# Strassen sums of x by accumulating DMA with one token half kept negative, memory's gains folded into ScalarE's rounding, and early loads issued at the start

## Chip, cores and metric

One core of one Trainium2 chip. The metric is device time in microseconds of one execution; lower is better. The kernel before took 919.43 us (median of 3 runs, 918.79 to 920.02).

## The reference, cut to what matters

One layer of a streaming encoder over 544 tokens (512 of a prompt, 32 of a running stream), width 2048, all in float32:

```python
h = rmsnorm(x, g_norm); proj = h @ w_in          # 2048 -> 6656
rq, rk, rv, rg, gu, gv, gg, aq, ag = split(proj)
ro = groupnorm(retention(rope(rq), rope(rk), rv)) * silu(rg)
go = gu * (tril(w_s) @ layernorm(gv) + b_s) * silu(gg)
ao = softmax(aq @ mem_k.T) @ mem_v * silu(ag)
out = x + concat([ro, go, ao]) @ w_out;  y = rmsnorm(out, g_final)
mem_k, mem_v = split(rmsnorm(mem_prompt, g_mem) @ w_mem_kv)   # 256 memory tokens
```

The memory's keys and values, the retention states and the normalised gate rows are outputs too.

## The kernel before, in words

Every large product is float32 by parts: an operand is split into an upper part, rounded to the matmul type (ScalarE, `copy`, L87), and a lower part, the remainder (VectorE, `tt`, L90); three matmuls (upper by upper, upper by lower, lower by upper) make one term. PE, DVE, ACT, POOL and SP are TensorE, VectorE, ScalarE, GpSimd and the sync engine's DMA queue.

The input projection runs by pairs of 128-column weight slices (`PAIRS`, L34: xa0 to xa3, then qk and vg by heads, gv, gg), the output projection as o0 to o7. Each pair is a 2 by 2 block product: K in two halves of 8 tiles, two weight slices, two halves of 272 tokens. xa0 and o0 do it with eight products (`plain`, L323); all others with seven (Strassen's form, `project`, L237), which needs four sums of the x blocks (S1 = 21 + 22, S3 = 11 - 21, S2 = S1 - 11, S4 = 12 - S2; block gi is token half g, K half i) and four sums of the weight blocks (`sources`, L173). One product is 24 matmuls of 272 columns (`multiply`, L221). A weight's two parts lie in tags `whi` and `wlo` with three buffers each; `ahead` (L209) makes the lower part of the next weight and begins (upper part) the one behind it.

Up to the end of xa0 the order on PE, DVE and ACT is the program's order by hand: `put` (L82) pins each instruction behind what was traced on its engine, until `fixed[0] = False` (L573). DMA starts are not pinned. After that the tile scheduler orders by readiness.

The stages before the first pair:

- Loads on SP (L407 to L412): memory tokens `mem` and key weights `wk` in pieces. The rest is issued between the key units, each behind the release of a buffer of the tag `raw` (three buffers): key piece 3, the constant table `ct`, the token-major x `xt` (only for its sums of squares), value weights `wv`, then x feature-major (`x`, L354, from `xT`), and xa0's weights (`load_half`, L166).
- Keys (L443 to L474): for 8 units, DVE multiplies memory by its gains (`gains_mem`, L416), ACT rounds weights and memory, DVE makes the remainders, ACT squares the memory (L432), PE does 24 matmuls.
- Values (L479 to L543): 8 units of 12 matmuls of 512 columns. In between, the sums of squares of memory and x become factors (`token_factors`, L292, with a power on POOL), spread over the partitions by diagonal matmuls (`rm_ps`, `r_ps`), copied to `rm_bc` and `r_bc`.
- x: `scale_x` (L524) multiplies each K tile by gain and token factor; `split_x` (L528) and `block` (L400) split the blocks into `A11`, `A21`, `A12`, `A22`.
- xa0 (`plain` with `between`, L553): the sums of x are DVE instructions over 128 x 2176 elements, at j = 3 and 5 and, for S4, in `last_sums` (L577). Block S2 follows at j = 5, S1 at j = 7; S3 and S4 in `last_sums`. ACT copies the results to `Xxa` (`pair`), from which head 0's scores `sc` are made (L601).

Of the kernel before, what the change touches and what calls it, by code (L numbers as in the profile page):

```python
# [8 lines left out]
F32 = mybir.dt.float32  # L9
# [5 lines left out]
P = 128  # L15
# [61 lines left out]
def step_kernel(ctx: ExitStack, tc: tile.TileContext, a, o):  # L77
# [95 lines left out]
    def sources(name, key):  # L173
# [12 lines left out]
        if key == "t3":  # L186
# [7 lines left out]
            f"o{NO - 1}": ("11", "21", "t2", "t1", "22", "t3", "t4")}  # L194
    units = [(n, key) for n in ORDER for key in FOUR.get(n, SEVEN)]
    begun, done = [], [0]

    def begin():

        if len(begun) < len(units):  # L200
            name, key = units[len(begun)]
            load_half(ORDER.index(name), 0)
            load_half(ORDER.index(name), 1)
            src = sources(name, key)
            u = unit(f"{name}{key}")
            copy(u[0], src)
            begun.append((src, u))

    def ahead():  # L209

        if done[0] < len(units):
            if done[0] == len(begun):
                begin()
            name, key = units[done[0]]
            src, u = begun[done[0]]
# [119 lines left out]


    with tc.tile_pool(name="mkv", bufs=1, reuse_waits="tile") as mkv, ExitStack() as ctx_x:
# [3 lines left out]
        with tc.tile_pool(name="pa", bufs=1, reuse_waits="tile") as pa:  # L341
            mem = [ap.tile([P, KS, MEM], F32, tag=f"12{u}", name=f"mem{u}") for u in "hl"]
            mg = [ap.tile([P, KS, MEM], F32, tag=f"22{u}", name=f"mg{u}") for u in "hl"]
# [3 lines left out]
            xk = [ap.tile([P, KS, T], F32, tag="S4", name="x0"), pb.tile([P, KS, T], F32, name="x1")]  # L347
# [5 lines left out]
            def load_x(k0, k1):  # L353
                nc.sync.dma_start(out=xk[k0 // KS][:, k0 % KS:k0 % KS + k1 - k0], in_=a["xT"][:, k0:k1])  # L354

            def load_kv(which, q, pieces=1):
                r = wp.tile([P, 4, 512], F32, tag="raw", name=f"{which}{q}", bufs=3)
# [54 lines left out]
            load_mem(12, 16)  # L412
            put(nc.vector.memset(ssx, 1.0))


            def gains_mem(u):  # L416
                if u < 8:
                    i, ks = u // 4, slice(u % 4 * 2, u % 4 * 2 + 2)
                    tt(mg[i][:, ks], mem[i][:, ks], gm[:, 2 * u:2 * u + 2].unsqueeze(2).to_broadcast([P, 2, MEM]), ALU.mult)

            ku = {}

            def key_unit(u):
                if u < 8:
                    i, ks = u // 4, slice(u % 4 * 2, u % 4 * 2 + 2)
                    w, src = unit(f"k{u}", [P, 2, 512]), wk[u // 2][:, u % 2 * 2:u % 2 * 2 + 2]
                    copy(w[0], src)
# [4 lines left out]
                    put(nc.scalar.activation(out=mem[i][:, ks], in_=mem[i][:, ks], func=AF.Square))  # L432
                    ku[u] = w

            vu, wv = {}, []
# [6 lines left out]
            gains_mem(0)  # L442
            key_unit(0)  # L443
            for u in range(8):
                key_unit(u + 1)
                if u == 5:
                    part0 = halve(mem[0], KS)
                elif u == 6:
                    value_unit(0)
                elif u == 7:  # L450
                    part1 = halve(mem[1], KS)
                    value_unit(1)
                    square_x(0)
                for k in range(2 * u, 2 * u + 2):
# [4 lines left out]
                if u == 1:  # L459
                    wk.append(load_kv("wk", 3))  # L460
                    nc.sync.dma_start(out=ct, in_=a["table"][:, 0:K_COS])
                    for t in (0, 1, 4):
                        load_tokens(t)
                elif u == 3:
                    wv.append(load_kv("wv", 0))
                    for t in (2, 3):
                        load_tokens(t)
                elif u == 5:
                    wv.append(load_kv("wv", 1))
                elif u == 7:  # L470
# [16 lines left out]
            square_x(1)  # L487
# [31 lines left out]
            copy(r_bc, ps[:, 0:T])  # L519
            value_unit(7)  # L520
            value(5)
            load_half(0, 1)

            def scale_x(i, k0, k1):  # L524
                for k in range(k0, k1):
                    stt(xk[i][:, k], xk[i][:, k], gn[:, KS * i + k:KS * i + k + 1], r_bc, ALU.mult, ALU.mult)

            def split_x(i, k0, k1):  # L528
                if k0 == 0:
                    new_block(f"1{i + 1}", "A")  # L530
                h = A[f"1{i + 1}"]
                split(h[0][:, k0:k1], h[1][:, k0:k1], xk[i][:, k0:k1, 0:TH])

            scale_x(0, 0, 4)
            split_x(0, 0, 4)
            value(6)
            scale_x(0, 4, 8)
# [6 lines left out]
            nc.sync.dma_start(out=o["cache_v"].rearrange("(m p) c -> p m c", p=P), in_=mv_p)  # L544
            put(nc.vector.tensor_scalar(out=gret, in0=gret, scalar1=0.5, scalar2=None, op0=ALU.mult))
            block("21", xk[0][:, :, TH:T])
# [4 lines left out]
            h11, h21, h12, h22 = xk[0][:, :, 0:TH], xk[0][:, :, TH:T], xk[1][:, :, 0:TH], xk[1][:, :, TH:T]  # L551

            def between(j):  # L553
# [514 lines left out]
def laid_out(i):  # L1068
# [21 lines left out]
    r["xT"] = feature_major(np.concatenate([i["x_prompt"][0], i["x_sample"][0]], 0))  # L1090
    r["xH"] = np.ascontiguousarray(r["xT"].reshape(P, KT, 2, TH).transpose(0, 2, 1, 3))
# [31 lines left out]
```

## Time and profile before

| | |
|---|---|
| median of 3 runs | 919.43 us |
| the profiled execution, its own time | 920.97 us |
| its span | 919.2 us |
| PE busy | 884.9 us, 96% |
| DVE busy | 716.4 us, 78% |
| ACT busy | 438.6 us, 48% |
| POOL busy | 17.3 us, 2% |
| mean granted clock of PE | 0.982 |
| moved by DMA | 126.51 MB |

Times in rows are microseconds from the span's start unless marked ns. PEld is TensorE's weight load, which overlaps PE. In brackets stands how long the engine sat idle before a row and what released it. PEclk is the granted clock as a share of full speed. Matmul ends are modelled, so a matmul's duration overlaps the next one's start.

### The profile page before, as it was taken

The numbers are of one execution on the slowest core, as the hardware profiler recorded it, in microseconds if no ns is written. First come the engines' busy times: TensorE is split into PE (matmuls) and PEld (weight loads), VectorE is DVE, ScalarE is ACT, GpSimd is POOL, SyncE is SP. The second block draws the span as 40 slices with busy tenths as digits, with TensorE's granted clock in tenths as the row PEclk, the third lists the DMA queues.
The fourth block names the chain that finished last, engine by engine and source line by source line (L and its number), as shares of the span: only waits on it lengthen the run. The fifth ranks groups of instructions, "written<-read, shape, count | busy, mean of one in ns | idle before, by whom it ended". The sixth has DMA issues, their size and how long they took to land.

```text
span 919.2 us, 16081 instructions
## 1 busy us (share of the span) xinstructions
PE 884.9 (96%) x6716; PEld 855.0 (93%) x6716; DVE 716.4 (78%) x1010; ACT 438.6 (48%) x648; POOL 17.3 (2%) x21
## 2 busy tenths in 40 slices
PE   8888799999999999999999999999999999999994
PEld 8767799989999999999999999999999999999993
DVE  6568996568678786969686968778898998777775
ACT  6635465555434444435344444433544845554540
POOL 0000000000000000000000000000100000000000
PEclk9998999999999999999999999999999999999997
DMA  9972133222322322323222231337645947233304
GB/s 355 378 281 81 46 127 111 100 66 95 116 73 92 101 105 101 105 101 105 101 88 71 88 113 64 106 108 261 223 159 183 363 171 260 92 96 119 109 1 194
DMA packets 36264, 126.51 MB, mean 138 GB/s; under 512 B 3584, under 2 KB 19072, under 8 KB 25568
## 3 DMA queue, kind: packets, MB, share of 16 engines
q1 hardware_dynamic: 35616, 124.39, 38.1%
q10 hardware_dynamic: 576, 1.11, 0.4%
q8 instruction: 52, 0.85, 0.4%
q14 instruction: 20, 0.16, 0.0%
HBM read 110.51 MB, written 14.97 MB: 137 GB/s over the span
## 4 chain that ended last, share of the span: by engine, by line
PE 80%; DVE 9%; DMA 4%; issue 2%; ACT 2%; POOL 1%; SPq 0%; POOLq 0%; DVEq 0%; ACTq 0%
PE o0p L96 3%; DMA wv<-in_wv 2%; PE xa2y L96 1%; PE gg1y L96 1%; PE vg6y L96 1%; PE vg7y L96 1%; PE vg3y L96 1%; PE vg2y L96 1%; PE qk5y L96 1%; PE qk3y L96 1%; PE qk7y L96 1%; PE qk4y L96 1%; PE qk1y L96 1%; PE o6y L96 1%; PE o4y L96 1%
## 5 line engine op out<-in xcount | busy, mean ns | idle before, releaser
L87 ACT ACTIVATE h_qk<-wqk 128x1024 fp32r<-128x1024 f32 x24 | 25.4, 1058 | 54.1 <-PE qk0y L96 3.7
L87 ACT ACTIVATE h_vg<-wvg 128x1024 fp32r<-128x1024 f32 x24 | 25.3, 1055 | 48.1 <-PE qk1z L96 4.4
L90 DVE TENSOR_TENSOR l_qk<-wqk,h_qk 128x1024 fp32r<-128x1024 f32 x24 | 29.3, 1222 | 23.0 <-ACT h_qk L87 23.0
L87 ACT ACTIVATE h_o<-wo 128x1024 fp32r<-128x1024 f32 x25 | 26.5, 1059 | 32.0 <-PE o3y L96 2.5
L90 DVE TENSOR_TENSOR l_o<-wo,h_o 128x1024 fp32r<-128x1024 f32 x25 | 30.5, 1222 | 7.0 <-ACT h_o L87 6.9
L90 DVE TENSOR_TENSOR l_vg<-wvg,h_vg 128x1024 fp32r<-128x1024 f32 x24 | 29.2, 1216 | 3.6 <-ACT h_vg L87 3.6
L90 DVE TENSOR_TENSOR l_v<-wv,h_v 128x1024 fp32r<-128x1024 f32 x8 | 9.8, 1225 | 16.1 <-ACT h_v L87 16.1
L90 DVE TENSOR_TENSOR l_xa<-wxa,h_xa 128x1024 fp32r<-128x1024 f32 x13 | 15.8, 1220 | 6.8 <-ACT h_xa L87 6.8
L87 ACT ACTIVATE zT<-zT,gall 128x272 f32<-128x272 f32 x32 | 15.8, 516 | 8.9 <-DVE last L90 8.4
L87 ACT ACTIVATE h_xa<-wxa 128x1024 fp32r<-128x1024 f32 x13 | 13.5, 1049 | 13.3 <-PE xa0p L96 4.6
L137 POOL TENSOR_TENSOR stats<-stats,mhalf 128x5 f32<-128x5 f32 x8 | 9.4, 1170 | 549.7 <-DVE stats L748 549.7
L87 ACT ACTIVATE h_gg<-wgg 128x1024 fp32r<-128x1024 f32 x12 | 12.6, 1056 | 13.0 <-PE gg2y L96 3.4
L90 DVE TENSOR_TENSOR l_gg<-wgg,h_gg 128x1024 fp32r<-128x1024 f32 x12 | 14.6, 1215 | 1.7 <-ACT h_gg L87 1.7
L90 DVE TENSOR_TENSOR cats<-cats 128x272 f32<-128x272 f32 x28 | 11.8, 431 | 3.4 <-DMA cats<-cat 3.1
L737 PE MATMUL po<-vN,sT 128*128 128x128 f32 (+1 forms) x80 | 14.2, 276 | 0.0
L610 ACT ACTIVATE pr<-sc,st 128x256 f32<-128x256 f32 (+1 forms) x20 | 9.0, 468 | 9.1 <-DVE st L607 9.1
L757 DVE TENSOR_SCALAR on<-po,stats 128x128 f32<-128x128 f32 (+1 forms) x40 | 13.3, 400 | 0.0
L87 ACT ACTIVATE h_v<-wv 128x1024 fp32r<-128x1024 f32 x8 | 8.3, 1052 | 10.3 <-DMA wv<-in_wv 7.8
L87 ACT ACTIVATE h_gv<-wgv 128x1024 fp32r<-128x1024 f32 x6 | 6.4, 1059 | 14.3 <-PE gv0z L96 4.4
L740 PE MATMUL po<-S,Xqk 128*128 128x128 f32 (+1 forms) x64 | 12.5, 277 | 0.0
L87 ACT ACTIVATE h_k<-wk 128x1024 fp32r<-128x1024 f32 x8 | 8.5, 1058 | 7.5 <-DMA wk<-in_wk 6.5
L722 PE MATMUL pu<-vN,kN 128*128 128x128 f32 (+1 forms) x80 | 11.7, 284 | 0.0
(1915 smaller groups left out, 3950.2 us busy)
## 6 DMA issues: line engine op xcount, KB each, us to landing
wqk<-in_w SPq DMA_DIRECT2D x16, 1024.0 KB, 4.8
wvg<-in_w SPq DMA_DIRECT2D x16, 1024.0 KB, 4.7
wo<-in_w SPq DMA_DIRECT2D x16, 1024.0 KB, 5.1
wxa<-in_w SPq DMA_DIRECT2D x8, 1024.0 KB, 5.4
wgg<-in_w SPq DMA_DIRECT2D x8, 1024.0 KB, 5.5
x<-in_xT SPq DMA_DIRECT2D x4, 1088.0 KB, 13.6
xt<-in_x SPq DMA_DIRECT2D x4, 1024.0 KB, 15.9
wv<-in_wv SPq DMA_DIRECT2D x4, 1024.0 KB, 15.0
```

Of the source, the lines that this page charges most:

```text
L87: put(nc.scalar.activation(out=out, in_=in_, func=AF.Copy, scale=scale))
L90: put(nc.vector.tensor_tensor(out=out, in0=in0, in1=in1, op=op))
L96: put(nc.tensor.matmul(out, lhsT=lhsT, rhs=rhs, start=start, stop=stop, **more))
L137: nc.gpsimd.tensor_tensor(out=out, in0=in_, in1=mhalf[0:n, 0:1].to_broadcast([n, in_.shape[1]]), op=ALU.pow)
L610: nc.scalar.activation(out=pr[0:n, t, :], in_=ps[0:n, (t - t0) * MEM:(t - t0 + 1) * MEM], func=AF.Exp, bias=st[0:n, 0, t:t + 1], scale=DH ...
L722: nc.tensor.matmul(pu[:, t * P:(t + 1) * P], lhsT=kN[0:n, t, :], rhs=v[0:n, t, :], start=True, stop=True)
L737: nc.tensor.matmul(po[0:n, t * P:(t + 1) * P], lhsT=sT[0:n, t * P:t * P + n], rhs=v[0:n, t, :], start=True, stop=(t == 0))
L740: nc.tensor.matmul(po[0:n, t * P:(t + 1) * P], lhsT=q[:, t * P:t * P + n], rhs=S[:, t - 1 if t < 4 else 4, :], start=False, stop=True)
L757: nc.vector.tensor_scalar(out=on[0:n, t, :], in0=po[0:n, t * P:(t + 1) * P], scalar1=s_[0:n, t, 0:1], scalar2=s_[0:n, t, 4:5], op0=ALU.sub ...
```

## The change

Four things are done. (1) x is loaded with its token halves apart (from `xH`), and the first half of the factors is copied with the sign turned, so that x blocks 11 and 12 are negative. All four sums of x then are plain additions and go as accumulating transfers from POOL's queue, two per sum. Weights that meet a negative block (`MINUS`: keys 11, 21, t3, 22) are rounded with the sign turned, in all pairs but xa0 and the output projection; their lower part is one scalar form instead of a subtraction. xa0's result is turned when it is copied out. (2) The memory's gains are applied by ACT's rounding copy (scale) and by a scalar form for the lower part; the products `mg` are gone. (3) All loads up to x's last quarter are issued at the start; key piece 3 and value piece 0 have places of their own. (4) The order of instructions in the key, value and xa0 stages is another; the eight products of xa0 come in another order; the writes of `cache_k` and `cache_v` come later.

```diff
+    MINUS = ("11", "21", "t3", "22")
...
-            copy(u[0], src)
-            begun.append((src, u))
-    def ahead():
+            sign = -1.0 if key in MINUS and name != "xa0" and name[0] != "o" else 1.0
+            copy(u[0], src, scale=sign)
+            begun.append((src, u, sign))
+    def ahead(more=True):
...
-            tt(u[1], src, u[0].bitcast(F32), ALU.subtract)
+            if sign > 0:
+                tt(u[1], src, u[0].bitcast(F32), ALU.subtract)
+            else:
+                stt(u[1], src, -1.0, u[0].bitcast(F32), ALU.mult, ALU.subtract)
...
-            begin()
+            if more:
+                begin()
...
-        for j, (k, c, g) in enumerate(((0, 0, 0), (0, 0, 1), (0, 1, 1), (0, 1, 0), (1, 0, 0), (1, 0, 1), (1, 1, 1), (1, 1, 0))):
+        for j, (k, c, g) in enumerate(((0, 0, 0), (0, 1, 0), (0, 1, 1), (0, 0, 1), (1, 0, 0), (1, 1, 0), (1, 1, 1), (1, 0, 1))):
...
+            wk.append(load_kv("wk", 3, 1, "22h"))
+            load_tokens(0)
+            load_tokens(1)
+            wv = [load_kv("wv", 0, 1, "22l")]
+            nc.sync.dma_start(out=ct, in_=a["table"][:, 0:K_COS])
+            load_tokens(4)
+            load_tokens(2)
+            wv.append(load_kv("wv", 1))
+            load_tokens(3)
+            load_x(0, 4)
+            wv.append(load_kv("wv", 2))
+            load_x(4, 8)
+            wv.append(load_kv("wv", 3))
+            load_half(0, 0)
+            load_x(8, 12)
+            load_half(0, 1)
+            load_x(12, 16)
...
+            def square_mem(u):
+                i, ks = u // 4, slice(u % 4 * 2, u % 4 * 2 + 2)
+                put(nc.scalar.activation(out=mem[i][:, ks], in_=mem[i][:, ks], func=AF.Square))
...
-                    copy(mm[i][0][:, ks], mg[i][:, ks])
-                    gains_mem(u + 1)
+                    for k in (k0, k0 + 1):
+                        copy(mm[i][0][:, k], mem[i][:, k], scale=gm[:, KS * i + k:KS * i + k + 1])
...
-                    tt(mm[i][1][:, ks], mg[i][:, ks], mm[i][0][:, ks].bitcast(F32), ALU.subtract)
+                    for k in (k0, k0 + 1):
+                        stt(mm[i][1][:, k], mem[i][:, k], gm[:, KS * i + k:KS * i + k + 1], mm[i][0][:, k].bitcast(F32),
+                            ALU.mult, ALU.subtract)
...
-                if u == 5:
+                if u == 4:
                     part0 = halve(mem[0], KS)
                 elif u == 6:
                     value_unit(0)
+                    square_x(0)
                 elif u == 7:
+                    value_unit(1)
                     part1 = halve(mem[1], KS)
-                    value_unit(1)
-                    square_x(0)
+                    square_x(1)
...
             value_unit(3)
+            square_x(2)
+            value(1)
             d = diagonals(rm, P, 2, pa, "rm_d")
             value_unit(4)
             square_x(3)
+            value(2)
+            to_all_partitions(ps, d)
+            value_unit(5)
+            copy(rm_bc, ps[:, 0:MEM])
+            r = token_factors(ssx[:, 0:5], "r")
+            value(3)
             for h in range(XH):
                 tt(mkT_p[:, h], kps[h][:, 0:MEM], rm_bc, ALU.mult)
             d = diagonals(r, P, 5, pa, "r_d")
             value_unit(6)
             value(4)
             ps = small("r_ps")
             to_all_partitions(ps, d)
-            copy(r_bc, ps[:, 0:T])
+            copy(r_bc[:, 0:TH], ps[:, 0:TH], scale=-1.0)
+            copy(r_bc[:, TH:T], ps[:, TH:T])
             value_unit(7)
+            scale_x(0, 0, 4)
             value(5)
             split_x(0, 0, 4)
+            ahead()
+            scale_x(0, 4, 8)
             value(6)
             split_x(0, 4, 8)
+            ahead(False)
             value(7)
-            ahead()
-            ahead()
+            block("21", xk[0][:, 1])
...
+            def add_to(x, y):
+                for k in range(0, KS, 4):
+                    nc.gpsimd.dma_start(out=x[:, k:k + 4], in_=y[:, k:k + 4], accum_op=ALU.add)
...
                 elif j == 3:
-                    tt(h22, h21, h22, ALU.add)
+                    add_to(h22, h21)
+                    add_to(h21, h11)
+                    add_to(h11, h22)
+                    add_to(h12, h11)
                 elif j == 5:
-                    tt(h21, h11, h21, ALU.subtract)
-                    tt(h11, h22, h11, ALU.subtract)
                     block("S2", h11)
...
-            plain("xa0", lambda c, g, ps: copy(pair[c][:, g * TH:(g + 1) * TH], ps[:, 0:TH]), between)
+            plain("xa0", lambda c, g, ps: copy(pair[c][:, g * TH:(g + 1) * TH], ps[:, 0:TH], scale=(-1.0, 1.0)[g]),
+                  between)
             def last_sums():
                 block("S3", h21)
                 yield
-                tt(h12, h12, h11, ALU.subtract)
                 yield
                 block("S4", h12)
```

## Rows read from the trace of the kernel before

**Rows 1.** The page, busy time of each engine, share of the span, instructions.
```profile
PE 884.9 (96%) x6716; PEld 855.0 (93%) x6716; DVE 716.4 (78%) x1010; ACT 438.6 (48%) x648; POOL 17.3 (2%) x21
```

**Rows 2.** Busy time by stretch: length, engines, granted clock, DMA share, GB/s.
```profile
7.30:32.95 25.65, 24.87 (x192) 24.27 (x192) 19.80 (x25) 15.21 (x23) 0.00 (x0) 0.93 1.02 376
32.95:65.90 32.95, 28.41 (x111) 22.08 (x110) 18.89 (x26) 19.65 (x23) 1.88 (x2) 0.90 0.87 352
65.90:100.50 34.60, 27.66 (x194) 26.90 (x195) 29.57 (x28) 16.89 (x19) 0.00 (x0) 0.90 0.27 89
100.50:114.84 14.34, 9.14 (x61) 7.73 (x60) 14.34 (x13) 7.10 (x10) 0.00 (x0) 0.99 0.03 9
114.84:919.20 804.36, 790.10 (x6140) 769.54 (x6140) 631.95 (x916) 376.83 (x573) 15.19 (x15) 0.99 0.36 125
```

**Rows 3.** Timeline of PE, matmuls behind idle time: start, us, instruction, [idle <-releaser].
```profile
45.99 1.01 PE L96 MATMUL rm_ps<-rm_d,ones 128*128 128x256 f32 x2 [2.81 <-DVE rm_d L90]
...
70.67 0.59 PE L96 MATMUL xa0p<-A11h,h_xa 128*128 128x272 f32 x1 [4.78 <-ACT h_xa L87]
...
72.19 0.60 PE L96 MATMUL xa0p<-A11h,l_xa 128*128 128x272 f32 x1 [0.70 <-DVE l_xa L90]
...
106.83 0.39 PE L96 MATMUL xa1x<-A12h,l_xa 128*128 128x272 f32 x1 [0.75 <-DVE l_xa L90]
...
114.84 0.59 PE L96 MATMUL xa1y<-AS2h,l_xa1t 128*128 128x272 f32 x1 [0.87 <-DVE l_xa1t L90]
```

**Rows 4.** Tile l_xa, a matmul group: ns min/median/max, first and last start.
```profile
L96 PE MATMUL xa0p<-A21h,l_xa x16: 287/289/291, 77.4 to 83.1; 128*128 128x272 f32 x16
```

**Rows 5.** Busy time by stretch, 48 to 52 us (columns as in rows 2).
```profile
48.00:52.00 4.00, 4.00 (x15) 3.20 (x14) 2.63 (x6) 3.11 (x4) 0.90 (x1) 0.79 0.08 33
```

**Rows 6.** Waits of SP's queue up to 130 us: total, times, longest.
```profile
SPq L506 <- DVE r L296: 12.1, 1, 12.1
```

**Rows 7.** Timeline of ACT, two upper parts behind idle time.
```profile
40.26 1.06 ACT L87 ACTIVATE h_v<-wv 128x1024 fp32r<-128x1024 f32 x1 [1.67 <-DMA wv<-in_wv]
...
80.27 1.06 ACT L87 ACTIVATE h_xa<-wxa 128x1024 fp32r<-128x1024 f32 x1 [4.61 <-PE xa0p L96]
```

**Rows 8.** Timeline of DVE, last value unit to block 21.
```profile
59.27 1.23 DVE L90 TENSOR_TENSOR l_v<-wv,h_v 128x1024 fp32r<-128x1024 f32 x1 [3.11 <-ACT h_v L87]
60.41 2.87 DVE L93 SCALAR_TENSOR_TENSOR x<-x,gall,r_bc 128x544 f32<-128x544 f32 x4
64.45 1.29 DVE L90 TENSOR_TENSOR A11l<-x,A11h 128x1088 fp32r<-128x1088 f32 x1 [1.18 <-ACT A11h L87]
...
74.69 2.49 DVE L90 TENSOR_TENSOR A21l<-x,A21h 128x1088 fp32r<-128x1088 f32 x2 [1.34 <-ACT A21h L87]
```

**Rows 9.** Tile x, ACT's rounding of a half block (columns as in rows 4).
```profile
L87 ACT ACTIVATE A11h<-x x2: 1109/1110/1112, 63.3 to 68.6; 128x1088 fp32r<-128x1088 f32 x2
```

**Rows 10.** Timeline of DVE, block 22, the first sum, weight 21 of xa1.
```profile
89.96 2.49 DVE L90 TENSOR_TENSOR A22l<-x,A22h 128x1088 fp32r<-128x1088 f32 x2
92.48 2.43 DVE L90 TENSOR_TENSOR x<-x,x 128x2176 f32<-128x2176 f32 x1
...
105.56 1.22 DVE L90 TENSOR_TENSOR l_xa<-wxa,h_xa 128x1024 fp32r<-128x1024 f32 x1
```

**Rows 11.** DMA issues: tile, count, KB each, median us from issue to landing.
```profile
zT<-in_xH SPq DMA_DIRECT2D x7, 544.0 KB, 6.4
out_y<-zT SPq DMA_DIRECT2D x7, 544.0 KB, 2.7
...
zT<-z0d SPq DMA_DIRECT2D x1, 544.0 KB, 4.4
```

**Rows 12.** Tile sc, head 0's scores (up to 130 us; columns as in rows 4).
```profile
L96 PE MATMUL sc<-mkT_p,Xxa x8: 377/379/381, 103.6 to 105.2; 128*128 128x256 f32 x8
```

**Rows 13.** Groups of DVE by form, 100 to 900 us: busy us, mean ns, idle.
```profile
L90 DVE TENSOR_TENSOR Xqk<-Xqk,cs 128x544 f32<-128x544 f32 x16 | 11.3, 706 | 0.0
...
L93 DVE SCALAR_TENSOR_TENSOR Xvg<-pt,gall,Xvg 128x544 f32<-128x544 f32 x8 | 6.1, 766 | 0.0
```

More of the change, by code (lines that the diff above doesn't have):

```diff
@@ L353, in load_x, with load_kv @@
             def load_x(k0, k1):
-                nc.sync.dma_start(out=xk[k0 // KS][:, k0 % KS:k0 % KS + k1 - k0], in_=a["xT"][:, k0:k1])
-            def load_kv(which, q, pieces=1):
-                r = wp.tile([P, 4, 512], F32, tag="raw", name=f"{which}{q}", bufs=3)
+                nc.sync.dma_start(out=xk[k0 // KS][:, :, k0 % KS:k0 % KS + k1 - k0], in_=a["xH"][:, :, k0:k1])
+            def load_kv(which, q, pieces=1, tag=None):
+                if tag:
+                    r = ap.tile([P, 4, 512], F32, tag=tag, name=f"{which}{q}")
+                else:
+                    r = wp.tile([P, 4, 512], F32, tag="raw", name=f"{which}{q}", bufs=3)
                 n = 4 // pieces
@@ new lines, in step_kernel, with key_unit @@
+            load_x(12, 16)
+            put(nc.vector.memset(ssx, 1.0))
+            ku = {}
+            def square_mem(u):
+                i, ks = u // 4, slice(u % 4 * 2, u % 4 * 2 + 2)
+                put(nc.scalar.activation(out=mem[i][:, ks], in_=mem[i][:, ks], func=AF.Square))
+            def key_unit(u):
+                i, k0 = u // 4, u % 4 * 2
+                if u < 8:
+                    w, src = unit(f"k{u}", [P, 2, 512]), wk[u // 2][:, u % 2 * 2:u % 2 * 2 + 2]
+                    if u:
+                        copy(w[0], src)
+                    for k in (k0, k0 + 1):
+                        copy(mm[i][0][:, k], mem[i][:, k], scale=gm[:, KS * i + k:KS * i + k + 1])
+                    if not u:
+                        copy(w[0], src)
@@ L430, in key_unit @@
                     tt(w[1], src, w[0].bitcast(F32), ALU.subtract)
-                    tt(mm[i][1][:, ks], mg[i][:, ks], mm[i][0][:, ks].bitcast(F32), ALU.subtract)
-                    put(nc.scalar.activation(out=mem[i][:, ks], in_=mem[i][:, ks], func=AF.Square))
+                    for k in (k0, k0 + 1):
+                        stt(mm[i][1][:, k], mem[i][:, k], gm[:, KS * i + k:KS * i + k + 1], mm[i][0][:, k].bitcast(F32),
+                            ALU.mult, ALU.subtract)
                     ku[u] = w
-            vu, wv = {}, []
+                if u:
+                    square_mem(u - 1)
@@ L485, in value, with scale_x, split_x @@
                                    start=(k == 0 and j == 0), stop=(k == KT - 1 and j == 2))
-            square_x(1)
+            def scale_x(i, k0, k1):
+                for k in range(k0, k1):
+                    stt(xk[i][:, :, k], xk[i][:, :, k], gn[:, KS * i + k:KS * i + k + 1], halves(r_bc), ALU.mult, ALU.mult)
+            def split_x(i, k0, k1):
+                if k0 == 0:
+                    new_block(f"1{i + 1}", "A")
+                h = A[f"1{i + 1}"]
+                split(h[0][:, k0:k1], h[1][:, k0:k1], xk[i][:, 0, k0:k1])
             value_unit(2)
@@ L518, in step_kernel @@
             to_all_partitions(ps, d)
-            copy(r_bc, ps[:, 0:T])
+            copy(r_bc[:, 0:TH], ps[:, 0:TH], scale=-1.0)
+            copy(r_bc[:, TH:T], ps[:, TH:T])
             value_unit(7)
+            scale_x(0, 0, 4)
             value(5)
[L522 to L534, printed above, removed]
             split_x(0, 0, 4)
+            ahead()
+            scale_x(0, 4, 8)
             value(6)
-            scale_x(0, 4, 8)
             split_x(0, 4, 8)
+            ahead(False)
             value(7)
-            ahead()
-            ahead()
+            block("21", xk[0][:, 1])
             for m in range(2):
                 copy(mv_p[:, m], vps[:, m * 512:(m + 1) * 512], scale=rm[:, m:m + 1])
-            nc.sync.dma_start(out=o["cache_v"].rearrange("(m p) c -> p m c", p=P), in_=mv_p)
-            put(nc.vector.tensor_scalar(out=gret, in0=gret, scalar1=0.5, scalar2=None, op0=ALU.mult))
-            block("21", xk[0][:, :, TH:T])
             first = const.tile([P, 2, T], F32, tag="cs", name="Xxa0")
             pair = first[:, 0, :], first[:, 1, :]
-            h11, h21, h12, h22 = xk[0][:, :, 0:TH], xk[0][:, :, TH:T], xk[1][:, :, 0:TH], xk[1][:, :, TH:T]
+            h11, h21, h12, h22 = xk[0][:, 0], xk[0][:, 1], xk[1][:, 0], xk[1][:, 1]
+            def add_to(x, y):
+                for k in range(0, KS, 4):
+                    nc.gpsimd.dma_start(out=x[:, k:k + 4], in_=y[:, k:k + 4], accum_op=ALU.add)
             def between(j):
@@ L560, in between @@
                     split_x(1, 4, 8)
+                    nc.sync.dma_start(out=o["cache_k"], in_=mkT_p)
                 elif j == 2:
@@ L572, in between @@
                     load_half(1, 1)
+                    nc.sync.dma_start(out=o["cache_v"].rearrange("(m p) c -> p m c", p=P), in_=mv_p)
+                    put(nc.vector.tensor_scalar(out=gret, in0=gret, scalar1=0.5, scalar2=None, op0=ALU.mult))
                     fixed[0] = False
-            plain("xa0", lambda c, g, ps: copy(pair[c][:, g * TH:(g + 1) * TH], ps[:, 0:TH]), between)
+            plain("xa0", lambda c, g, ps: copy(pair[c][:, g * TH:(g + 1) * TH], ps[:, 0:TH], scale=(-1.0, 1.0)[g]),
+                  between)
             def last_sums():
```

47 lines of the change are left out of this document (4 added, 43 removed).

## Prediction

> **What bounds the kernel now.** I read the page first, then busy time by stretch, then the idle times of TensorE, and last the queues of DVE, ACT and SP around each of these. The page has PE busy for 884.9 us, 96% of the span [rows 1]; the question is where the other 34 us lie and what the clock costs besides. By stretch [rows 2], everything behind 114.84 us is TensorE's: 790.1 of 804.4 us, at a granted clock of 0.99. What is won must therefore be won before 114.84, where the first projection pair's third product (weight sum t2 by block S2) gets going: whatever makes that point earlier makes the end earlier, because all that follows is a queue of products. Ahead of it are four stages. Keys (7.30 to 32.95): PE 24.87 of 25.65, so TensorE's own. Values (to 65.90): PE 28.4 of 33, 4.5 idle. First projection xa0 (to 100.50): PE 27.7 of 34.6, DVE 29.6. Then 100.50 to 114.84: PE 9.1 of 14.3 and DVE 14.34 of 14.34, the one stretch where DVE is wholly full. The idle times of TensorE [rows 3] say what ends the gaps: rm_d (2.81), the rounding of x and of the first weights (4.78 and 0.70), l_xa (0.75), t2's low part (0.87). After the 4.78 the matmul at 72.19 takes 0.60 us where 0.29 is usual [rows 3, 4]: the lower of the clock's two levels, 1.2 in place of 2.4 GHz. One product is 24 matmuls, 3.02 us at the full clock (16 low-part matmuls, which two products have, start between 77.4 and 83.1 [rows 4]); the first one here took some 5.
>
> **Key stage: no gain.** DVE loses 8 gain products and pays 16 scalar forms of half the width for 8 low parts; ACT splits 8 copies in two. Both have room (DVE 19.8 and ACT 15.2 of 25.65 [rows 2]) and PE has none, so PE's matmuls hide it; the first matmul may start a few tenths earlier. Without that cover, 8 more instructions on ACT would cost some 1 to 2 us.
>
> **Early loads: little by themselves.** The DMA engines are at 1.02 in the key stage and 0.87 in the value stage [rows 2]; what idles is one hole, 48 to 52 us at 0.08 [rows 5], while SP sat 12.1 us in front of the cache_k write (L506) [rows 6]. From the start through the fourth wv piece both kernels move the same 17.4 MB, so that piece cannot land earlier. The change only reorders: at the key stage's 376 GB/s [rows 2] 1 MB takes 2.8 us; wv1, which landed just before 40.26 [rows 7], comes one piece earlier, at 37.5; wv2 comes behind a piece of tokens and 1.1 MB of x, at about 46. The hole's 4 us go to x's second half and xa0's weights, which are not late in either kernel. On SP, x(8,12) is now behind xa0's first weights and x(12,16) behind its second; these wait for raw buffers that value units 3 and 5 free, at about 43 and 51 us, while earlier pieces still fill the queue. The writes of cache_k and cache_v go behind all that, and nobody waits for them.
>
> **Value stage: 3.0 us.** wv0 now goes ahead of the two small tables, so value(0) follows the keys at once (1.7 of the 4.5 idle), and the diagonals of the memory factors are used behind value(2), so the 2.81 goes. Against that, the halving of the second memory part stands behind value unit 1 on DVE, and the memory sums wait some 2.3 us for it. The path to the token factors is now ACT's: wv2 lands at 46.0, value unit 4 rounded 47.05, fourth square 48.95, unit 5 50.0; then DVE's low part 51.2, factors and POOL's power 52.6, diagonals 53.4, PE 54.5, r_bc 55.3, unit 7 56.3, its low part 57.4. So scaling begins at 57.4 where it is 60.41 [rows 8].
>
> **xa0's blocks: 5.85 us at the last read of x.** Before, DVE waits twice 1.18 us for ACT between 60.41 and A21l's end at 77.2 [rows 8]. After, the first weight's low part fills time there and A21 no longer stands behind mv_p: four scalings 2.8, A11h 1.1 [rows 9], A11l 1.25, weight 1.15, scalings 2.8, A11h 1.1, A11l 1.25, weight 1.15, A21l 2.4 are 15 us, to 72.4. PE does half of product 0 early and resumes at 68.8. With 2.0 us lost to the lower clock, as before, products 0, 1 and 2 end at 78.4 (68.8 + 1.5 + 2.0 + 3.02 + 3.02), product 3 at 81.4. Here the new product order bites: the upper part of weight 22 needs one of three buffers, and w12's is free first, after product 2, w11's after product 3; before, it was free after product 1, at 80.27 [rows 7]. ACT's later copies are queued behind that wait: weight 79.4, A12h 81.5; DVE: A12l 83.0, weight 84.2, A22l 86.6, where it was 92.45 (89.96 + 2.49 [rows 10]). Nothing reads x22 after that, so the sums may begin.
>
> **The sums.** Before, 22.4 us of DVE lie between 92.45 and 114.84: four sums of 2.43, blocks, weights. After, the four are gone (9.7 us). S2 needs three sums one behind the other (each writes what the one before it reads), each as two transfers of 544 KB from POOL's queue, and then S2's upper part 1.1, its low part 1.25, weight 21's low part 1.22, two sums for t2 (1.22 each), t2's rounding 1.06 and low part 1.22 [rows 7, 9, 10]: 8.3 us. S2 is pinned, so ACT and DVE stand at it; behind it wait weight 21's low part, hence xa1's product 21, and the evacuation of xa0's last two results. No row shows an accumulating transfer or one from POOL. Rows of the same size [rows 11]: 2.7 us from issue to landing (to memory), 4.4 (from memory, a buffer written by the kernel), 6.4 (input, beside weights). I take 4.4, which like the sums writes SBUF and is mostly alone. Two reads for one write argue for more, staying within SBUF for less. The bounds are 2.7 below and 8.8 above (twice 4.4, the two halves of a step one after the other). So t2 starts at 86.6 + 13.2 + 8.3 = 108.1, 6.7 us earlier.
>
> The Trainium skill (DMA: Bandwidth & Descriptors, "Anatomy of one DMA — SWDGE (gpsimd) path") fits a transfer issued by GpSimd to 2.0 us plus its bytes at 436 GB/s; by that a step is 3.3 us and the sum 3.3 us better, 911.8. It is a fit for plain copies, and no row here shows it.
>
> **Work that loses its cover: 2.4 us.** Head 0's scores (8 large matmuls from 103.6 on [rows 12] and 2 small ones, to 106.08, where the 0.75 of [rows 3] begins) now fill time in which PE would wait. They need both halves of xa0's first result; its second half is now product 7, which ACT copies out behind S2 and t2's rounding. So they fall behind t2, where PE is full.
>
> **Minus signs: nothing.** 100 low parts become scalar forms: 766 ns against 706 at 544 columns [rows 13], at most 0.1 us each at 1024, 10 us of DVE at the worst over 804 us in which it is busy for 632 [rows 2]. PE's backlog covers it; without that it is up to 10 us.
>
> **Sum.** 6.7 − 2.4 = 4.3 us. The profiled execution took 920.97 us (span 919.2 and 1.8 around it), which makes 916.7; the median shown is 919.43, 1.5 lower, which makes 915.1. A measurement of this kernel tells 0.2%, 1.84 us, from no change.
>
> **Rivals.** *The transfers land fast*, 2.7 a step: three times 1.7 better, 910.0. For it: nearly nothing else is on the DMA then, 0.03 [rows 2]. *They cost what was saved*: at 5.8 a step the gain is nil, 919.4, and from 5.2 to 6.4 it can't be told. The same comes if weight 22 takes w11's buffer, free one product later: 918.1; or if POOL can put out each step only once DVE's instruction ends, three times 1.25: 918.9. On the last the Trainium skill (SBUF — State Buffer, "SBUF: two separate sides") has GpSimd's descriptors wait while DVE runs an operation that uses both ports for one tensor; DVE's rows in this stretch read two tensors, so by the page it would not happen. *The sums become the bound*: S2 stands in the queues of ACT and DVE, and from 6.4 us a step on the chain costs more than DVE's sums did. At 8.8 it is three times 4.4 later, 928.3: slower. For it: two transfers a step, the destination read as well; against: 544 KB is 1.4 us at the rate of the key stage. *The early loads bring nothing* is in the sum already.
>
> **How the numbers follow.** Forecast 0.38, fast landing 0.20, nothing to tell 0.20, slower 0.22; so faster 0.58, same 0.20, slower 0.22. The range 908.5 to 922.0 takes in the fast rival and 1.5 us less of lower clock on one side, the 6.4 row (921.1) and little more on the other; it leaves out most of the 8.8 case. The faster cases alone are 909 to 917.6.
>
> **What would show it.** Right: scaling of x from 57.4, A22l's end near 86.6, POOL issues from 85 on and landings 4 to 5 us later, ACT and DVE idle before S2 until about 100, t2's matmuls near 108, the scores behind them, no idle PE later. Wrong: A22l behind 89 (the buffer), steps of over 6 us (the sums), or PE idle behind t2 because S1, S3 or S4 is late.

## The result, and the profile after

The changed kernel takes **927.04 us** (median of 4 runs, 926.67 to 927.53); the kernel before, beside it, 919.72 (4 runs, 918.79 to 920.57). The ratio is 1.0082 [1.007, 1.0094]: 0.8% slower, clear of the interval, where 915.1 and a range up to 922.0 were forecast. The profiled execution took 927.09 us, its span is 925.3.

The page's busy times after answer to [rows 1]: DVE has 12.7 us less work and PE as much as before.

```profile
PE 883.9 (96%) x6716; PEld 854.3 (92%) x6716; DVE 703.7 (76%) x1006; ACT 440.6 (48%) x657; POOL 24.5 (3%) x29
```

Busy time by stretch after, cut near the same events as [rows 2] (columns as there):

```profile
7.30:32.65 25.35, 24.06 (x193) 23.67 (x193) 19.35 (x28) 19.23 (x31) 0.00 (x0) 0.93 1.02 388
32.65:62.10 29.45, 25.31 (x114) 20.11 (x112) 17.97 (x25) 19.75 (x26) 1.89 (x2) 1.00 1.00 392
62.10:99.40 37.30, 29.81 (x192) 28.72 (x193) 22.23 (x24) 13.04 (x16) 3.70 (x4) 0.86 0.48 125
99.40:120.43 21.03, 10.22 (x59) 8.75 (x58) 12.80 (x11) 10.02 (x12) 3.51 (x4) 0.76 0.70 133
120.43:925.30 804.87, 789.40 (x6143) 768.28 (x6142) 631.16 (x917) 375.82 (x572) 15.20 (x15) 0.99 0.36 125
```

The cuts are not quite the same: 120.43 is the first matmul of t2's product, 114.84 was its third, the first that reads t2's low part (the first ran before at 113.45, see below). The third is now at 120.78, 5.9 us later than before, and behind it the stretch is as long as it was (804.52 against 804.36), so the reading that the end hangs on t2's product holds. By PE's timeline the last value matmul ends 4.2 us earlier than before (61.68 for 65.89), pair xa1 begins only 1.2 us earlier (99.22 for 100.37), and the stretch from there to t2's low part takes 7.1 us more. That stretch was full of DVE before; now DVE works 12.80 of its 21.03 us. DVE no longer has too much to do there: it waits.

The timeline of PE after, idle times and t2's first matmul, answers to [rows 3]:

```profile
38.39 0.61 PE L96 MATMUL rm_ps<-ones,meml 128*128 128x1 f32 x4 [2.51 <-DVE meml L90]
...
84.60 0.39 PE L96 MATMUL xa0p<-A12h,h_xa 128*128 128x272 f32 x1 [2.28 <-ACT A12h L87]
85.93 0.59 PE L96 MATMUL xa0p<-A12l,h_xa 128*128 128x272 f32 x1 [0.94 <-DVE A12l L90]
...
112.74 0.60 PE L96 MATMUL xa1x<-A12h,l_xa 128*128 128x272 f32 x1 [9.21 <-DVE l_xa L93]
118.82 1.13 PE L96 MATMUL sc<-mkT_p,Xxa 128*128 128x256 f32 x4 [1.60 <-ACT Xxa L87]
...
120.43 0.39 PE L96 MATMUL xa1y<-AS2h,h_xa1t 128*128 128x272 f32 x1
...
120.78 0.29 PE L96 MATMUL xa1y<-AS2h,l_xa1t 128*128 128x272 f32 x1
```

The 9.21, where the same matmul waited 0.75 before [rows 3], is where the loss shows. It names weight 21's low part (l_xa), but that instruction waited in DVE's queue behind S2's low part, and S2 waited for the transfers. The timeline of DVE shows this (answering to [rows 8, 10]):

```profile
56.28 2.87 DVE L93 SCALAR_TENSOR_TENSOR x<-x,gall,r_bc 128x544 f32<-128x544 f32 x4
...
69.06 2.49 DVE L90 TENSOR_TENSOR A21l<-x,A21h 128x1088 fp32r<-128x1088 f32 x2
...
79.33 1.29 DVE L90 TENSOR_TENSOR A12l<-x,A12h 128x1088 fp32r<-128x1088 f32 x1 [3.87 <-ACT A12h L87]
80.54 2.86 DVE L93 SCALAR_TENSOR_TENSOR x<-x,gall,r_bc 128x544 f32<-128x544 f32 x4
...
86.93 2.49 DVE L90 TENSOR_TENSOR A22l<-x,A22h 128x1088 fp32r<-128x1088 f32 x2
...
110.26 1.29 DVE L90 TENSOR_TENSOR AS2l<-x,AS2h 128x1088 fp32r<-128x1088 f32 x1 [1.71 <-ACT AS2h L87]
111.47 1.22 DVE L93 SCALAR_TENSOR_TENSOR l_xa<-wxa,h_xa 128x1024 fp32r<-128x1024 f32 x1
```

POOL's timeline holds the eight issues of the four sums, the first released by A22l, the later ones by the landing that they need:

```profile
88.53 2.07 POOL L562 DMA_DIRECT2D x<-x  x2 [37.42 <-DVE A22l L90]
95.09 0.87 POOL L562 DMA_DIRECT2D x<-x  x1 [4.49 <-DMA x<-x]
98.42 0.90 POOL L562 DMA_DIRECT2D x<-x  x1 [2.47 <-DMA x<-x]
...
103.67 0.87 POOL L562 DMA_DIRECT2D x<-x  x1 [1.75 <-DMA x<-x]
```

And ACT's timeline shows where the third step ends (the second half of S2's upper part starts at 109.11) and what follows:

```profile
109.11 1.11 ACT L87 ACTIVATE AS2h<-x 128x1088 fp32r<-128x1088 f32 x1 [1.61 <-DMA x<-x]
115.14 2.12 ACT L87 ACTIVATE AS<-x 128x1088 fp32r<-128x1088 f32 x2 [4.91 <-DVE xa1T L90]
117.16 1.03 ACT L87 ACTIVATE h_xa1t<-xa1T 128x1024 fp32r<-128x1024 f32 x1
```

A22l ends at 89.42 (86.93 + 2.49), so the three steps took 109.11 − 89.42 = 19.7 us, 6.6 each on average. They are not alike: counted to the landing of each step's second half (which releases the issues at 98.42 and 103.67, and S2's rounding at 109.11), they took 9.0, 5.3 and 5.4 us.

### The profile page after: what moved, and what is told of

Read it like the earlier page. It is cut to its first block, busy times and chain, and to the rows that moved or that the text cites. A ratio compares the mean times of both kernels' runs of the same rounds, so it can differ in the third digit from the quotient of the medians.

```text
span 925.3 us, 16112 instructions
## 1 busy us (share of the span) xinstructions
PE 883.9 (96%) x6716; PEld 854.3 (92%) x6716; DVE 703.7 (76%) x1006; ACT 440.6 (48%) x657; POOL 24.5 (3%) x29
## 3 DMA queue, kind: packets, MB, share of 16 engines
q0 software_dynamic: 1152, 4.46, 2.5%
q10 hardware_dynamic: 576, 1.11, 0.4%
## 4 chain that ended last, share of the span: by engine, by line
PE 76%; DVE 4%; DMA 3%; ACT 2%; issue 1%; POOL 1%; SPq 0%; POOLq 0%; DVEq 0%; ACTq 0%
PE o0p L96 3%; PE xa2y L96 1%; PE o2y L96 1%; PE gg1y L96 1%; PE vg2y L96 1%; PE vg7y L96 1%; PE vg3y L96 1%; PE vg6y L96 1%; PE qk2y L96 1%; PE qk6y L96 1%; PE qk5y L96 1%; PE qk1y L96 1%; PE o6y L96 1%; PE o4y L96 1%; PE o3y L96 1%
## 5 line engine op out<-in xcount | busy, mean ns | idle before, releaser
L93 DVE SCALAR_TENSOR_TENSOR l_qk<-wqk,h_qk 128x1024 fp32r<-128x1024 f32 x24 | 29.4, 1223 | 22.7 <-ACT h_qk L87 22.7
L90 DVE TENSOR_TENSOR l_o<-wo,h_o 128x1024 fp32r<-128x1024 f32 x25 | 30.6, 1222 | 5.7 <-ACT h_o L87 5.7
L93 DVE SCALAR_TENSOR_TENSOR l_vg<-wvg,h_vg 128x1024 fp32r<-128x1024 f32 x24 | 29.2, 1217 | 3.6 <-ACT h_vg L87 3.6
L87 ACT ACTIVATE h_xa<-wxa 128x1024 fp32r<-128x1024 f32 x13 | 13.6, 1050 | 20.1 <-PE xa0p L96 8.8
L90 DVE TENSOR_TENSOR l_k<-wk,h_k 128x1024 fp32r<-128x1024 f32 x8 | 9.8, 1223 | 9.3 <-ACT h_k L87 9.3
L93 DVE SCALAR_TENSOR_TENSOR l_xa<-wxa,h_xa 128x1024 fp32r<-128x1024 f32 x9 | 11.0, 1221 | 7.1 <-ACT h_xa L87 7.1
L93 DVE SCALAR_TENSOR_TENSOR l_gg<-wgg,h_gg 128x1024 fp32r<-128x1024 f32 x12 | 14.6, 1217 | 2.0 <-ACT h_gg L87 2.0
L90 DVE TENSOR_TENSOR ss<-ss,sq 128x272 f32<-128x272 f32 x26 | 10.8, 436 | 2.9 <-ACT ss L966 2.9
L969 ACT ACTIVATE sq<-zT 128x272 f32<-128x272 f32 x26 | 10.3, 416 | 4.8 <-DVE zT L90 4.8
```

Of the source, the lines that this page charges most:

```text
L87: put(nc.scalar.activation(out=out, in_=in_, func=AF.Copy, scale=scale))
L90: put(nc.vector.tensor_tensor(out=out, in0=in0, in1=in1, op=op))
L93: put(nc.vector.scalar_tensor_tensor(out=out, in0=in0, scalar=scalar, in1=in1, op0=op0, op1=op1))
L969: nc.scalar.activation(out=s, in_=z, func=AF.Square)
```

## Experiments

Theory: the accumulating transfers, which everything up to t2 waits for, cost more than DVE's sums. Rivals: the other parts of the change lose the time (DVE's order, the minus signs, the order of products), or it is POOL's queue. All are compared with the kernel before on the same chip (its medians 919.66 to 920.10).

**The transfers against DVE, all else as changed.**

```diff
-                for k in range(0, KS, 4):
-                    nc.gpsimd.dma_start(out=x[:, k:k + 4], in_=y[:, k:k + 4], accum_op=ALU.add)
+                tt(x, x, y, ALU.add)
...
+                add_to(h12, h11)
```

(the second and third sum go back to their place behind product 5, the fourth to its place before S4; S2 is pinned where it was.)

> The changed kernel with its four x sums back on VectorE (as additions, at the places of the kernel before); signs, loads and order stay. Theory (three accumulating steps of 6.6 us, 89.4 to 109.1, are the loss): VectorE needs from A22l's end at 89.4 the 22.4 us that it needed before, so t2 is back at about 112 where it was 120.4, and the time is 918 to 920. Rival (the new order of products and instructions is the loss, whatever adds): above 924, with t2 still near 120.

Measured: 919.34 us, ratio 0.9991 [0.9981, 1.0]. So the transfers at that place are the whole loss, some 8 us (1.0082 against 0.9991), and the rest of the change, as it stands, is worth next to nothing. The other way round, the transfers and signs put into the kernel before:

> The kernel before with the signs and the accumulating transfers alone: loads, memory gains, order of stages and of products as before. Theory: A22l ends at 92.4 as before, three steps of 6.6 us bring S2's last half to about 112, t2 to 120 to 123: 925 to 929, so the transfers alone are the whole loss or more. Rival (only in the new order do they hurt): within 2 us of 920.

Its diff is the new add_to, MINUS with the other turned signs, and the layout of x by halves, nothing else. Measured: 929.79 us (4 runs, 925.61 to 930.37), 1.0092 [1.0068, 1.0116], just above what was expected. Its POOL timeline, first and last issue:

```profile
91.93 2.06 POOL L561 DMA_DIRECT2D x<-x  x2 [40.63 <-DVE A22l L90]
...
114.03 0.89 POOL L561 DMA_DIRECT2D x<-x  x1 [2.17 <-DMA x<-x]
```

From the first issue to the last are 22.1 us, in the changed kernel 109.50 − 88.53 = 21.0: the same chain, in another surrounding.

**Why e1 wins so little.** Its A22l ended at 88.13, 4.3 us before that of [rows 10]. PE's timeline shows where that went, first that of the kernel before:

```profile
113.45 0.39 PE L96 MATMUL xa1y<-AS2h,h_xa1t 128*128 128x272 f32 x1 [3.58 <-ACT h_xa1t L87]
```

then that of e1:

```profile
110.33 0.39 PE L96 MATMUL xa1y<-AS2h,h_xa1t 128*128 128x272 f32 x1 [3.58 <-ACT h_xa1t L87]
...
110.90 1.92 PE L96 MATMUL sc<-mkT_p,Xxa 128*128 128x256 f32 x4
...
113.75 0.60 PE L96 MATMUL xa1y<-AS2h,l_xa1t 128*128 128x272 f32 x1
```

t2's product began 3.1 us earlier, but six of the ten score matmuls, which PE had done in idle time before [rows 12], came into it, in part at the lower clock (1.2 GHz; granted 0.66 on average from 110 to 115 us), and the product went on with t2's low part at 113.75, only 1.1 us earlier than before (114.84).

**Is it the adding, or POOL?** Plain copies in the place of the sums, from POOL and from SP:

```diff
-                    nc.gpsimd.dma_start(out=x[:, k:k + 4], in_=y[:, k:k + 4], accum_op=ALU.add)
+                    nc.gpsimd.dma_start(out=x[:, k:k + 4], in_=y[:, k:k + 4])
```

> The same eight POOL transfers as plain copies (the x sums are left out, so S1 to S4 hold copies). Measures what adding costs. If reading the destination is what makes a transfer slow: 3 to 4 us from issue to landing where it is 5.6, a step near 4.5 us, time near 921. If the issue by POOL and the completion make it: 5 us or more, step above 5.5 us, time 925 to 927.

> The same plain copies from SP's queue (sums left out). Measures what POOL's issue costs. If it is the issue: 2.7 to 3.5 us from issue to landing, a step of 3.5 us, time 917 to 920. If any copy within SBUF of this size takes 5 us, as on POOL's queue: 925 to 927.

Measured, one execution each: 922.72 and 921.11 us. The first is near the 921 named for a step of 4.5 us; the second lies between its two ranges, though its transfers took 3.0 us. The DMA view from 84 to 115 us (queue: packets, MB, share of the 16 engines' time; issues: count, KB, median us to landing), first the changed kernel:

```profile
q0 software_dynamic: 1152, 4.46, 74.5%
...
x<-x POOLq DMA_DIRECT2D x8, 544.0 KB, 5.6
```

the plain copies by POOL in the same stretch:

```profile
q0 software_dynamic: 1152, 4.46, 35.1%
...
x<-x POOLq DMA_DIRECT2D x8, 544.0 KB, 3.1
```

and by SP:

```profile
x<-x SPq DMA_DIRECT2D x8, 544.0 KB, 3.0
```

The same 1152 packets and 4.46 MB take 74.5% of 31 us when they add and 35.1% when they copy: 193 GB/s against 410 (4.46 MB over 23.1 and 10.9 us). Adding halves the rate. Two halves in flight share that rate; by it a step of 1.11 MB would take 5.8 us (an estimate), and the second and third, which begin while the step before still runs, took 5.3 and 5.4. POOL isn't the reason, 3.1 against 3.0. The Trainium skill (DMA: Bandwidth & Descriptors, "Anatomy of one DMA — SWDGE (gpsimd) path") has 2.0 us plus the bytes at 436 GB/s, by which 544 KB take 3.3 us (an estimate): the plain copy's 3.1 agrees, the 5.6 does not. The chain of plain copies by POOL shows in three timelines (DVE, POOL twice, ACT):

```profile
88.76 2.49 DVE L90 TENSOR_TENSOR A22l<-x,A22h 128x1088 fp32r<-128x1088 f32 x2
...
98.64 0.54 POOL L562 DMA_DIRECT2D x<-x  x1 [2.25 <-DMA x<-x]
...
101.86 0.54 POOL L562 DMA_DIRECT2D x<-x  x1 [1.36 <-DMA x<-x]
...
104.84 1.11 ACT L87 ACTIVATE AS2h<-x 128x1088 fp32r<-128x1088 f32 x1 [0.25 <-DMA x<-x]
```

From A22l's end (91.25) to the second half of S2's upper part (104.84) it took 13.6 us, 4.5 a step on average: by the count used above 7.4, 3.2 and 3.0. So of the 19.7 us adding makes 6.1 (1.6 in the first step, 2.0 and 2.5 in the others), and the first step is the long one with plain copies too.

Does the low rate need the company of xa2's 1 MB weight load? Two accumulating transfers on a nearly idle DMA are seen in e10 below. Keeping the load away in the changed kernel was tried too:

```diff
-        load_half(i + 1, 0)
+        load_half(i + 1, 0, nc.gpsimd if name == "xa1" else None)
```

> The changed kernel with the 1 MB load of xa2's first weights issued by POOL behind the four sums instead of by SP at 87.1 us, so that no other load runs beside the transfers. Theory (the first step took 8 to 9 us because it shared the DMA engines with that load; without it 5.6 to 6): t2 2 to 3 us earlier, 924 to 925.5. Rival (accumulating transfers start slowly by themselves, the load is nothing to them): 926.5 to 927.5.

Measured: 929.53 us, 1.0109 [1.0095, 1.0124], which no theory expected, and it isn't the experiment that was meant. POOL's timeline shows that the load was issued ahead of the sums, not behind them:

```profile
86.55 0.74 POOL L171 DMA_DIRECT2D wxa<-in_w  x1 [36.76 <-ACT A22h L87]
87.40 0.87 POOL L562 DMA_DIRECT2D x<-x  x1
```

So it shared the engines with the first step again. No run here has the chain without that load. The load's packets took 10.4% of the 31 us, 3.2 us of the 16 engines; how much of that the first step lost can only be estimated, below, from e10's pair.

**Do the minus signs cost?** e1 without signs, its sums by subtraction:

```diff
-    MINUS = ("11", "21", "t3", "22")
+    MINUS = ()
```

> e1_dve_sums without the minus signs: x positive, sums by subtraction on VectorE, all lower parts as plain subtractions. Theory (100 scalar forms cost nothing, PE covers them): within 0.1% of e1, 919.3. Rival (they slow VectorE by up to 0.1 us each and PE waits for some): 1 to 5 us below e1.

Measured: 919.15 us, 0.9998 [0.9989, 1.0007]: nothing, as e1.

**DVE's order.** e1 with one line moved: x's last four scalings ahead of A12's low part.

```diff
                     scale_x(1, 0, 4)
+                    scale_x(1, 4, 8)
                     split_x(1, 0, 4)
...
-                    scale_x(1, 4, 8)
                     split_x(1, 4, 8)
```

> e1_dve_sums with the second four scalings of x's second half moved in front of the first A12 split, so that they don't stand behind VectorE's wait for A12h. Theory (VectorE's order there cost 2.8 us of A22l's end and two gaps of PE, 2.26 and 0.92): A22l ends near 85.3 where it is 88.1, t2 near 108, gain over e1 2 to 3 us: 916 to 917.5. Rival (ACT, which waits for product 2 to free weight 12's buffer, sets A12 anyway): A22l and the time as in e1, 919.3.

Measured: 915.19 us, 0.9943 [0.993, 0.9957], 4.2 below e1 and more than expected. DVE's timeline of e5:

```profile
71.81 5.66 DVE L93 SCALAR_TENSOR_TENSOR x<-x,gall,r_bc 128x544 f32<-128x544 f32 x8
78.51 2.49 DVE L90 TENSOR_TENSOR A12l<-x,A12h 128x1088 fp32r<-128x1088 f32 x2 [1.04 <-ACT A12h L87]
...
82.06 2.49 DVE L90 TENSOR_TENSOR A22l<-x,A22h 128x1088 fp32r<-128x1088 f32 x2
```

All eight scalings fall in the time in which DVE had waited 3.8 us for A12h; A22l ends at 84.55, 3.6 earlier than in e1, and PE's idle times of 2.3 and 0.9 in front of A12 are gone. The kernel before has its scalings in the old order too, and DVE waited 1.26 us for A12h there; what the one line would win in it was not run. The same line in the changed kernel:

> The changed kernel with one line moved: x's last four scalings stand ahead of A12's low part on DVE. In e5 against e1 the same move gave 4.15 us with DVE's sums. Theory (the transfers start as much earlier as A22l ends earlier, some 3.6 to 4.9 us, and t2 with them): 922 to 924. Rival (the first step is slow because a 1 MB weight load shares its time; it meets the load elsewhere and gains or loses): 919 to 921.5 or 925 to 927.

Measured: 923.26 us, 1.0036 [1.0023, 1.005], 3.8 below the changed kernel and within the theory's range. The transfers start 3.9 us earlier (84.64 for 88.53), as the theory had it, but the third step lands only 2.7 earlier (106.42 for 109.11): the first step took 9.9 us (85.52 to 95.41) where it was 9.0. Why it did was not followed.

**The place of the wait, and the order of products.** Block S2 behind product 7 in the changed kernel:

```diff
-                elif j == 5:
-                    block("S2", h11)
                 elif j == 7:
+                    block("S2", h11)
                     block("S1", h22)
```

> The changed kernel with block S2 made behind product 7 instead of behind product 5, so that weight 21's low part, t2's sums and the copies of xa0's last results no longer stand behind the wait; the transfers stay. If the place of the wait is half of the loss: S2 lands as before at about 109, is split by 111.5, t2 starts near 112 in place of 120.4, and the scores go into idle time: 917 to 920. If the length of the chain alone decides: t2 not before 118, time within 2 us of 927.

Measured: 922.14 us, 1.0028 [1.0017, 1.0038]: 4.9 of the loss is weight 21's low part and the scores standing behind S2 in the queues. It was to be 2 us less; a new idle time of 5.29 us stood in front of product t1 (113.69), whose rounding of t1 now came behind S2's second half and S1 on ACT.

e5 with the last four products in the old order, so that xa0's first result is whole two products earlier (S2 stays behind product 5):

```diff
-        ... (1, 0, 0), (1, 1, 0), (1, 1, 1), (1, 0, 1))):
+        ... (1, 0, 0), (1, 0, 1), (1, 1, 1), (1, 1, 0))):
```

> e5 with the last four products of xa0 in the order (1,0,0), (1,0,1), (1,1,1), (1,1,0), as the kernel before had it. Theory (head 0's scores lost their cover because their second half is product 7): the scores run before t2 again, 2.4 us of PE work in idle time: 1 to 2.4 us below e5. Rival: product 5 now needs A22, PE waits for it and t2 is late anyway: equal to e5 or slower.

Measured: **913.12 us**, 0.9927 [0.9914, 0.9939], 2.1 below e5 and the lowest median here. PE's timeline has all scores back in their old place, eight in 1.89 us as before, with t2's low part at 107.11:

```profile
95.90 1.89 PE L96 MATMUL sc<-mkT_p,Xxa 128*128 128x256 f32 x8
...
107.11 0.59 PE L96 MATMUL xa1y<-AS2h,l_xa1t 128*128 128x272 f32 x1 [0.78 <-DVE l_xa1t L90]
```

**Can the transfers pay at all?** The changed kernel, transfers and all, with these three repairs (the early scalings, S2 behind product 7, the old order of the last products):

> The changed kernel, its four sums still by accumulating transfers, with the two other losses taken away: the scaling of x's last four rows of blocks ahead of A12's low part (as in e5) and block S2 behind product 7, with the order of the last four products of before (as in e6). Theory (each transfer is hidden if its step's wait stands where TensorE has other work; A22l ends near 84.5, S2 lands near 104, t2 starts near 107 to 109): 914 to 917 us, 1 to 4 us above e6's 913.1. Rival (the transfers cost several us wherever they stand, since the last of three steps sets t2): 918 to 921. Other rival (they free 9.7 us of DVE and so beat DVE's sums): below 912.5.

Measured: 914.64 us, 0.9948 [0.9936, 0.9961]; the interval overlaps that of e6. Timelines of PE, then ACT:

```profile
98.16 1.89 PE L96 MATMUL sc<-mkT_p,Xxa 128*128 128x256 f32 x8
...
107.79 0.59 PE L96 MATMUL xa1y<-AS2h,h_xa1t 128*128 128x272 f32 x1 [7.19 <-ACT xa1u L87]
```

```profile
104.34 1.11 ACT L87 ACTIVATE AS2h<-x 128x1088 fp32r<-128x1088 f32 x1 [1.22 <-DMA x<-x]
105.36 2.09 ACT L87 ACTIVATE AS1h<-x 128x1088 fp32r<-128x1088 f32 x2
107.36 0.38 ACT L87 ACTIVATE xa1u<-xa1y 128x272 f32<-128x272 f32 x1
```

Weight 21, the weight sums and the scores now go on while the transfers run. What is left is one idle time of 7.19 us, and t2's low part is multiplied 1.3 us later than in e6 (108.41 for 107.11). Well placed, transfers and DVE's sums come out nearly even. The 9.7 us taken from DVE buy nothing, because t2 now hangs on ACT's queue: S2's second half waits for the last landing, and the copy xa1u that t2 needs stands behind it and behind S1. S2's low part was ready at 106.78, 1.0 us before t2 began; a kernel with that copy ahead of S1 was not run.

One sum alone by transfer, the fourth, in e6:

```diff
+                    for k in range(0, KS, 4):
+                        nc.gpsimd.dma_start(out=h12[:, k:k + 4], in_=h11[:, k:k + 4], accum_op=ALU.add)
...
-                add_to(h12, h11)
```

> e6 (DVE's sums, scaling early, old order of the last four products, S2 behind product 7) with one sum alone by accumulating transfers: the fourth, which S4 reads and which isn't on the way to t2. Theory (2.4 us of DVE between S3 and t2's low part go, nothing waits for the landing): 910.5 to 912.3. Rival (DVE has slack there, or S4 then gets ahead of t2's rounding on ACT): as e6, 912.6 to 914.

Measured: 913.78 us, 0.994 [0.9927, 0.9952]. (In e6, and so in this run, S2 stands behind product 5, not 7 as the expectation says.) The rival holds: no gain over e6. t2's low part was multiplied 0.7 us earlier (106.40 against 107.11), but a new idle time, which e6 doesn't have, came behind it:

```profile
112.12 0.39 PE L96 MATMUL xa1y<-AS3h,h_xa1t 128*128 128x272 f32 x1 [1.06 <-ACT xa1u L87]
```

Its DMA view from 92 to 104 us has two accumulating transfers with only 0.13 MB of another queue beside them:

```profile
q0 software_dynamic: 288, 1.11, 51.0%
q1 hardware_dynamic: 272, 0.13, 3.8%
...
x<-x POOLq DMA_DIRECT2D x2, 544.0 KB, 6.1
```

1.11 MB took 51% of 12 us, 6.1 us of all 16 engines, or 182 GB/s. So the low rate is that of adding; the weight load doesn't make it. The pair's two halves took 4.9 and 7.3 us from issue to landing, the slowest of the changed kernel, in its first step, 8.4. By these two numbers the load cost the first step some 1 us (an estimate); the rest of its length may be that no step before it was under way when it began (not tested apart).

## Why the prediction was wrong, point by point

The predicted span is 919.2 − 4.3 = 914.9. The misses add up to the measured one: A22l's end +2.8, the three steps +6.5, from the last landing to t2's low part +3.4 (11.7 where 8.3 was forecast), the stretch behind it −2.2 (2.4 longer expected, 0.2 seen: 804.52 less 804.36); unrounded they make 10.4, and 914.9 + 10.4 = 925.3. Two of the three signs of being wrong that were named came: A22l behind 89, though not by the buffer (weight 22 was rounded at 77.24, behind product 2, as worked out), and steps of over 6 us.

- **The step that failed most: the price of an accumulating step, 4.4 us.** It measured 6.6 on average (9.0, 5.3, 5.4). The row taken [rows 11] was a single plain transfer of 544 KB. Plain copies in the same place took 4.5 on average, so that price came out right for copying, but by luck: 4.5 is the mean of a long first step (7.4) and two short ones (3.2, 3.0), which the working didn't tell apart. Adding is 6.1 of the 6.5 us missed: it halves the rate, and with two halves in flight the rate, not the latency, is the price. "Two reads for one write argue for more" was written and then not priced. The rate of the key stage, 376 GB/s, used against the slower rival, belonged to plain loads.
- **A22l at 86.6 failed too: 89.4.** Everything up to weight 22 came as worked out, some 1 us earlier: scaling from 56.28 (predicted 57.4), A21l's end 71.55 (72.4), weight 22's upper part 77.24 (78.4, at the end of product 2). But the working put A12's two halves side by side. The program has x's last four scalings behind the first half's low part, which waits 3.87 us for ACT; their 2.86 us then hold up the second half. One moved line gave 4.2 us in e5 and 3.8 in e11.
- **8.3 us behind the landing: 11.7.** S4's upper part (2.12 at 115.14) stands ahead of t2's rounding on ACT, 2.0 us. It stood there in the kernel before too (ACT's timeline below), and the working left it out. The other 1.3 us are six of the scores, which went ahead of t2 on PE (t2's low part was ready at 119.46, its first matmul ran at 120.78).

```profile
110.34 2.11 ACT L87 ACTIVATE AS<-x 128x1088 fp32r<-128x1088 f32 x2 [6.35 <-DVE x L90]
```

- **The scores do not fall behind t2.** Four of the ten ran in idle time (at 102.50), six ahead of t2 (at 118.82). Behind t2 PE has a new idle time of 1.05 us (at 125.02, for ACT's copy xa1u), and t2's product from its low part on took 2.78 us at a granted clock of 1.00 (2.4 GHz), where before it took 4.25 at 0.64, most of it at 1.2 GHz. By these two the stretch would be 0.4 shorter; it is 0.2 longer, and the other 0.6 us was not followed.
- **Right:** the end hangs on t2's start; S2 in the queues of ACT and DVE makes the transfers everybody's wait; the new order of products costs most of the scores their cover (e6 wins 2.1 us where 2.4 was the price); the 2.81 of rm_d goes and a new wait for the memory sums comes (2.3 predicted, 2.51 seen); the minus signs are free (l_qk in the scalar form 1223 ns over 24, as a subtraction before 1222); x's scaling starts 4.1 us earlier (56.28 for 60.41) where 3.0 was forecast.
- **The rivals.** "The sums become the bound" is what happened, though its price of 8.8 a step was too high: by the measured 6.6 alone the span would be 914.9 + 6.5 = 921.4, 2.2 over that of before, and the other misses made it 925.3. "POOL can put out each step only once DVE's instruction ends" fell: the issues behind the first are released by landings. "Fast landing" at 2.7 fell.

## What to carry to other kernels

Price an accumulating transfer by its rate, not by a copy's latency, price the first step of a chain apart, and add up the whole chain: three dependent steps of 1.1 MB took 19.7 us (9.0, 5.3, 5.4) in place of 7.3 us of DVE's work. Work handed to a slower but free resource helps only if what waits for it stands behind all that doesn't, in each in-order queue; here the place of that wait and one line of DVE's order were worth more than the four sums. When a stretch is full of one engine, first ask whether its order lets it wait just before: the same sums on DVE, reordered, gave the lowest time, 913.12 us, and the transfers, reordered, 914.64.

## What the runs showed of the hardware that was not expected

- Accumulating transfers within SBUF ran at 182 to 193 GB/s, counted over the busy time of the 16 engines, plain ones at 410: 5.6 us against 3.1 for 544 KB. The Trainium skill (DMA: Bandwidth & Descriptors, "Rules for kernel authors") says that an accumulate reads its destination and writes it later, which fits a halved rate; no run here shows the two reads.
- A transfer issued from POOL took as long as one from SP (3.1 and 3.0 us, plain); POOL spends 0.87 us on issuing an accumulating one, and 0.54 on a plain one in e3.
